# The last six row tiles of an FFN output product, regrouped into seven block products

## The chip, the cores and the metric

The kernel runs on one core of a Trainium2 chip. The metric is device time in microseconds (us): the median of three runs. Beside the runs there is one profiled execution, whose trace gives the start and the duration of every instruction on each engine: PE (TensorE, matrix products; PEld is its weight load), DVE (VectorE), ACT (ScalarE), POOL (GpSimd), and SP, whose queue issues most transfers.

## What is computed

Two layers of an encoder on 512 tokens of width 1024. Each layer is a token mixer of three branches, then an FFN with a gate, each followed by a residual sum and a layer norm. Only the end of the FFN matters here:

```python
u = jnp.einsum('bsd,df->bsf', x, w_ffn_in[l])
u_gate, u_up = jnp.split(u, 2, axis=-1)
ffn = jnp.einsum('bsf,fd->bsd', jax.nn.silu(u_gate) * u_up, w_ffn_out[l])
x = _layer_norm(DEEPNORM_ALPHA * x + ffn, ln2_g[l], ln2_b[l])
```

The hidden width is 2816, which is 22 row tiles of 128. So the FFN's output product is (512 tokens x 2816) times (2816 x 1024).

## The kernel before

**Products.** All values are float32. A product of two float32 operands is carried by splitting each into a high and a low part and adding three matmuls, high by high, high by low and low by high (`mm3`, lines 121 to 124). A weight block is therefore loaded by SP into a staging buffer (pool `wst`, 4 buffers), cast to its high part by ACT and reduced to its low part by a DVE subtraction (`Wt.split`, lines 154 and 155; `Staged`, lines 259 and 260). The pairs live in the pool `wsp`, with 3 buffers (`AHEAD`): the block of an item can be split only when the item three places ahead of it has left PE.

**Seven products instead of eight.** A group of row tiles of `w_ffn_out` is cut in two halves by rows (`kh` tiles each) and in two halves by columns (512 each); the tokens are cut in two halves of 256. A plain product of such a 2x2 by 2x2 arrangement takes eight block products. `fout_items` (line 1316) takes seven, named m1, y, x, m2, v, g and h, on sums of blocks. A block product is `product` (line 337): for each token tile `j` of 128 (two of them), `kh` times three matmuls into one PSUM bank. The sums of weight blocks are made by transfers that add to a staging buffer (`more`, line 177, on POOL's queue). The class `Chain` (line 191) holds one such buffer `a` from m1 to h, and another, `c`, for g. The sums of activation blocks are made by `Quarters.parts` and `Quarters.sums` (lines 279 and 289) on ACT and DVE, through the scheduled function `s_hid` (line 1214). Each finished block product is added into the residual tiles `z` by `plus` (line 1305), one DVE instruction of 128x512 for each use. There are eight `z` tiles: four token tiles `t`, two column halves `hf` each. m1 is added to one place and kept by an ACT copy, y is kept by an ACT copy, x takes five DVE instructions for each token tile (a subtraction, an addition, three of `plus`), g is added at two places, m2, v and h at one.

**The plan before.** `GROUPS` has two groups of eight row tiles, 0 to 7 (`o`) and 8 to 15 (`w`). The row tiles 16 to 21 (`REST`) are multiplied plainly by `fout_rest` (line 1367): for column half 0, a block of four and a block of two row tiles, whose four banks are added to `z` at the end; for column half 1, `chase`, which finishes one token tile after the other with 18 matmuls and closes the tile's norm behind each. In layer 1 (the last), closing a token tile is `Norm.finish` (line 475): `bn_stats` is done by `plus` with `final`, then an aggregate, a sum, a power on POOL, two DVE instructions that subtract the mean and multiply by the gain, two that multiply by the inverse deviation and add the bias, and the transfers of the result. In layer 0 it is `Norm.normalise` (line 488), which has two DVE instructions behind the power; then `Norm.transposes` (line 497) and `to_T` (line 517) turn the token tiles 0 and 1 for the next layer, and its first products follow (`u_first`, `halves`, line 711, with the other two token tiles turned by `hook`).

**The order.** The work is a list of items (line 1404). `run_items` (line 554) walks it: it fetches the weight blocks of the items up to two places ahead, runs the item, and runs the groups of functions that hang on the item between its products or after them (`between`). A scheduler in the language then orders the instructions of each engine from that order and from what is ready; on the chip each engine runs its own list in order.

Of the kernel before, what the change touches and what calls it, by code (L numbers as in the profile page):

```python
# [15 lines left out]
ALU = mybir.AluOpType  # L16
# [4 lines left out]
NT = S // P  # L21
# [8 lines left out]
FT = FFN // P  # L30
# [17 lines left out]
AHEAD = 3  # L48
NSTAGE = 4


GROUPS = [(0, 4), (8, 4)]
REST = 16


@with_exitstack
def trunk(ctx, tc, x_in, xT_in, w_in, ret_norm_g, da_norm_g, lq1, lk1, lq2, lk2, w_a, w_b, w_c, b_merge, w_out,
# [25 lines left out]
    def bank(name="ps"):  # L83
        return psp.tile([P, 512], F32, tag="ps", name=name)
# [31 lines left out]
    def split(pr, src, cols=slice(None), scale=None):  # L116

        part_hi(pr.hi[:, cols], src, scale)
        part_lo(pr.lo[:, cols], src, pr.hi[:, cols], scale)
# [71 lines left out]
    class Chain(Halves):  # L191
# [23 lines left out]

        def h(self):
            return self.block(self.__dict__.pop("a"))

    class Close(Halves):

# [144 lines left out]
    def proj_N(act, wts, t, ps, k0=0, start=True, stop=True):  # L365

        sl = slice(P * t, P * t + P)
        rows = [(wt, k) for wt in wts for k in range(wt.nk)]
        for i, (wt, k) in enumerate(rows):
            a = act[k0 + i]  # L370
            mm3(ps, a.hi[:, sl], a.lo[:, sl], wt.hi[:, k], wt.lo[:, k], start and i == 0, stop and i == len(rows) - 1)

    def rows_of(w, c, k0=0, nk=KT):

        return [([w[P * k:P * min(k + 4, k0 + nk), c:c + 512]], min(4, k0 + nk - k)) for k in range(k0, k0 + nk, 4)]
# [80 lines left out]
    def bcast_rows(src):  # L456

        r = [g(name="bc") for _ in range(2)]
        for hf in range(2):
            nc.sync.dma_start(r[hf], src[:, 512 * hf:512 * hf + 512].to_broadcast([P, 512]))  # L460
        return r
# [80 lines left out]
    def item(specs, fn, *groups):  # L542

        items.append((specs, fn, groups))
# [62 lines left out]
    def layer(l):  # L607
# [595 lines left out]
        def ffn_done(i, pg, pu):  # L1203
            t = g(name="fth")
            nc.scalar.activation(t, pg, AF.Tanh, scale=0.5)
            nc.vector.scalar_tensor_tensor(t, t, 1.0, pg, op0=ALU.add, op1=ALU.mult)
            nc.vector.tensor_mul(t, t, pu)  # L1207
            if i >= REST:
                hid[i] = Pair("hid")
                split(hid[i], t, scale=0.5)  # L1210
            else:
                hid[i] = t

        def s_hid(k):

            def fn():
                r0, kh = GROUPS[1]
                t1, t2 = hid[r0 + k], hid[r0 + kh + k]
                hid[r0 + k], hid[r0 + kh + k] = Quarters(), None
                hid[r0 + k].parts(t1, t2, 0.5)  # L1220
                hid[r0 + k].sums(t1, t2, 0.5)
            return fn
# [58 lines left out]
        def u_fin(pb):  # L1281

            return u_two(Chain(w_ffn_in[l], 0, 4, (512 * pb, FFN + 512 * pb)), x1q,
                         functools.partial(gate_half, pb), functools.partial(gated, pb))
# [20 lines left out]
        def plus(t, hf, ps, op, final=False):  # L1305

            z = x1["z"][t][hf]
            if (t, hf) in x2["fresh"]:
                x2["fresh"].remove((t, hf))
                nc.vector.scalar_tensor_tensor(z, z, ALPHA, ps, op0=ALU.mult, op1=op)  # L1310
            else:
                nc.vector.tensor_tensor(z, z, ps, op=op)  # L1312
            if final:
                x2["n"].stats(t, hf)

        def fout_items(gi):

            r0, kh = GROUPS[gi]
            hv = Chain(w_ffn_out[l], r0, kh)
            w = {}  # L1320

            def run(name, j, wt):
                return product([hid[r0 + k] for k in range(kh)], name, j, wt)

            def m1(wt):
                if gi == 0:
                    load_res(saved[2 * l])
                    x2["fresh"] = {(t, hf) for t in range(NT) for hf in range(2)}
                for j in range(2):
                    ps = run("m1", j, wt)  # L1330
                    w[j] = g(name="w")
                    nc.scalar.copy(w[j], ps)
                    plus(j, 0, ps, ALU.add)

            def y(wt):
                for j in range(2):
                    ps = run("y", j, wt)
                    w["y", j] = g(name="wy")
                    nc.scalar.copy(w["y", j], ps)

            def x(wt):
                for j in range(2):
                    ps = run("x", j, wt)
                    u = w.pop(j)
                    nc.vector.tensor_sub(u, ps, u)
                    plus(2 + j, 0, u, ALU.subtract)
                    nc.vector.tensor_add(u, u, w.pop(("y", j)))
                    plus(2 + j, 1, u, ALU.add)
                    plus(j, 1, u, ALU.add)

            def one(name, i, hf, op):
                def fn(wt):
                    for j in range(2):
                        plus(2 * i + j, hf, run(name, j, wt), op)
                return fn

            def gg(wt):
                for j in range(2):
                    ps = run("g", j, wt)
                    plus(2 + j, 1, ps, ALU.add)  # L1360
                    plus(2 + j, 0, ps, ALU.subtract)

            return {"c": hv.ahead_c, "m1": ([hv.m1], m1), "y": ([hv.y], y), "x": ([hv.x], x),
                    "m2": ([hv.m2], one("m2", 0, 0, ALU.add)), "v": ([hv.v], one("v", 0, 1, ALU.add)),
                    "g": ([hv.g], gg), "h": ([hv.h], one("h", 1, 0, ALU.add))}

        def fout_rest(hf):


            banks = {}  # L1370
            specs = rows_of(w_ffn_out[l], 512 * hf, REST, FT - REST)

            def block(kb):
                def fn(wt):
                    if kb == 0:
                        x2["n"] = Norm(x1["z"], v["g2"], v["b2"], bcast_rows(ln2_g[l:l + 1]),
                                       bcast_rows(ln2_b[l:l + 1]), xTs[l + 1], out if last else saved[2 * l + 1], xfs[l + 1])
                        banks[0] = [bank("pf") for _ in range(NT)]
                    end = kb == len(specs) - 1
                    for t in range(NT):  # L1380
                        proj_N(hid, [wt], t, banks[0][t], REST + 4 * kb, kb == 0, end)
                        if end:
                            plus(t, 0, banks[0][t], ALU.add, True)
                return fn

            def chase(*wts):
                n = x2["n"]
                for t in range(NT):
                    ps = bank("pf")
                    proj_N(hid, wts, t, ps, REST)  # L1390
                    if t in (1, 2) and not last:
                        n.transposes(t - 1)
                    plus(t, 1, ps, ALU.add, True)
                    if last:
                        n.finish(t)
                    else:
                        n.normalise(t)
                        if t == 2:
                            n.to_T(0)

            return [([sp], block(kb)) for kb, sp in enumerate(specs)] if hf == 0 else [(specs, chase)]

        p, q, o, w = u_fin(0), u_fin(1), fout_items(0), fout_items(1)
        for (specs, fn), *groups in [
            (u_ffn_first([8, 9]), [s_natural(0)], [s_x1(0)]), (u_ffn(10), [s_x1(1), s_x1(2)], [s_x1(3), s_natural(1)]),
            (p["m1"], [s_natural(2)], [p["c"], s_natural(3)]), (u_ffn(11),), (p["y"],), (p["m2"],),
            (p["v"],), (p["x"],), (u_ffn(12), [], [s_turn(0, 0)]), (p["g"],), (p["h"],),
            (q["m1"], [], [q["c"]]), (u_ffn(13), [s_turn(0, 1)]), (q["y"],), (q["m2"],),
            (q["v"],), (q["x"],), (u_ffn(14), [], [s_turn(1, 0)]), (q["g"],), (q["h"], [s_ready(0)], [s_ready(1)]),
            (o["m1"], [], [s_turn(1, 1)]), (u_ffn(15), [s_twins(0)], [s_twins(1), o["c"]]), (o["m2"],), (o["y"],), (u_ffn(16),),  # L1410
            (o["v"],), (o["x"],), (u_ffn(17),), (o["g"], [], [s_hid(0)]), (o["h"], [], [s_hid(1)]), (u_ffn(18), [s_hid(2)], [s_hid(3)]),
            (w["m1"],), (u_ffn(19), [], [w["c"]]), (w["m2"],), (w["y"],), (u_ffn(20),),
            (w["v"],), (w["x"],), (u_ffn(21),), (w["g"],), (w["h"],),
        ]:
            item(specs, fn, *groups)
        for it in fout_rest(0) + fout_rest(1):
            item(*it)

        def hook(b):
            x2["n"].transposes_of(1, b)  # L1420
# [56 lines left out]
```

## Time and profile before

| | us |
|---|---|
| median of three runs | 1895.63 (1895.56 to 1895.76) |
| the profiled execution | 1896.34 |
| its span, first to last instruction | 1894.5 |
| PE busy in the span | 1881.4 |
| DVE busy in the span | 1355.1 |
| ACT busy in the span | 946.2 |
| mean granted TensorE clock | 0.997 of full |

The span is 1.8 us shorter than the profiled execution's own time, which in turn is 0.7 us above the median of the runs. All times of day in this document are microseconds from the start of the span. A row of the timeline gives start, duration, engine, line, operation, what is written from what, the shape, how many instructions are merged into the row, and in brackets how long the engine stood idle before it and what released it. Durations of neighbouring instructions on one engine overlap, so what a queue can do is read from the distance of starts.

### The profile page before, as it was taken

How to read it: one execution, taken by the hardware profiler on the slowest of the kernel's cores; microseconds unless marked ns; L12 is line 12 of the kernel's file. 1: busy time of each engine (PE TensorE's matmuls, PEld its weight loads, DVE VectorE, ACT ScalarE, POOL GpSimd, SP SyncE). 2: the span in 40 equal slices, each digit the busy share in tenths (PEclk: the TensorE clock that was granted, in tenths of full speed). 3: DMA queues.
4: the chain of work that ended last, by engine and by line, in shares of the span. 5: the costliest groups of instructions: out<-in, count | busy, mean ns of one | idle time of the engine just before them, and what ended most of it. 6: DMA issues, size and time to landing. Idle time of an engine off the chain costs nothing. (4 is left out here: it accounts for less than half of the span.)

```text
span 1894.5 us, 24166 instructions
## 1 busy us (share of the span) xinstructions
PE 1881.4 (99%) x9170; PEld 1584.9 (84%) x9170; DVE 1355.1 (72%) x2159; ACT 946.2 (50%) x1575; POOL 113.9 (6%) x141
## 2 busy tenths in 40 slices
PE   9999999999999999999999999999999999999998
PEld 7888888888888888888898888888888898888886
DVE  6788867577765866786687788666776668667866
ACT  5555555566634444543255546555765344344430
POOL 2000000000000000000010000000000000000000
PEclk9999999999999999999999999999999999999999
DMA  9585443332155686765475944533322637777561
GB/s 282 170 268 152 122 159 108 122 122 68 57 186 147 156 178 169 207 156 127 139 190 171 285 113 145 169 104 95 123 79 73 205 101 175 181 179 196 139 153 45
DMA packets 239348, 285.11 MB, mean 150 GB/s; under 512 B 8580, under 2 KB 147936, under 8 KB 239232
## 3 DMA queue, kind: packets, MB, share of 16 engines
q1 hardware_dynamic: 215232, 237.01, 38.1%
q0 software_dynamic: 24000, 46.56, 14.4%
q8 instruction: 72, 1.18, 0.3%
q14 instruction: 44, 0.36, 0.1%
HBM read 260.42 MB, written 23.12 MB: 150 GB/s over the span
## 5 line engine op out<-in xcount | busy, mean ns | idle before, releaser
L122 PE MATMUL pt<-xTh,wh 128*128 128x512 f32 (+1 forms) x1328 | 497.2, 375 | 2.3 <-ACT wh L154 2.0
L124 PE MATMUL pt<-xTh,wl 128*128 128x512 f32 (+1 forms) x1328 | 494.0, 372 | 0.0
L123 PE MATMUL pt<-xTl,wh 128*128 128x512 f32 (+1 forms) x1328 | 493.9, 372 | 0.0
L154 ACT CAST wh<-st 128x1024 fp32r<-128x1024 f32 (+1 forms) x236 | 220.2, 962 | 210.4 <-PE pt L123 91.1
L155 DVE TENSOR_TENSOR wl<-st,wh 128x1024 fp32r<-128x1024 f32 (+1 forms) x236 | 257.4, 1111 | 81.0 <-ACT wh L154 75.0
L260 DVE TENSOR_TENSOR wl<-st,wh 128x2048 fp32r<-128x2048 f32 x98 | 224.4, 2290 | 117.2 <-ACT wh L259 116.8
L122 PEld LDWEIGHTS pt<-xTh,wh 128*128 128x128 f32 x1328 | 250.1, 189 | 44.3 <-ACT wh L154 2.5
L124 PEld LDWEIGHTS pt<-xTh,wl 128*128 128x128 f32 x1328 | 250.5, 189 | 43.9
L123 PEld LDWEIGHTS pt<-xTl,wh 128*128 128x128 f32 x1328 | 250.9, 189 | 41.9
L259 ACT CAST wh<-st 128x2048 fp32r<-128x2048 f32 x98 | 187.5, 1913 | 157.4 <-PE pf L124 73.9
L124 PE MATMUL pf<-wh,xTl 128*128 128x512 f32 x240 | 93.4, 389 | 0.0
L123 PE MATMUL pf<-wl,xTh 128*128 128x512 f32 x240 | 93.4, 389 | 0.0
L122 PE MATMUL pf<-wh,xTh 128*128 128x512 f32 x240 | 93.4, 389 | 0.0
L122 PE MATMUL pf<-wh,s43h 128*128 128x512 f32 x192 | 75.5, 393 | 0.1
L122 PE MATMUL pf<-wh,s12h 128*128 128x512 f32 x192 | 74.9, 390 | 0.0
L123 PE MATMUL pf<-wl,s43h 128*128 128x512 f32 x192 | 74.8, 389 | 0.0
L124 PE MATMUL pf<-wh,s12l 128*128 128x512 f32 x192 | 74.7, 389 | 0.0
L123 PE MATMUL pf<-wl,s12h 128*128 128x512 f32 x192 | 74.7, 389 | 0.0
L124 PE MATMUL pf<-wh,s43l 128*128 128x512 f32 x192 | 74.2, 390 | 0.0
L382 ACT COPY sw<-pt 32x512 f32<-32x512 f32 (+1 forms) x96 | 55.7, 580 | 29.2 <-PE pt L124 28.0
L1207 DVE TENSOR_TENSOR fth<-fth,pt 128x512 f32<-128x512 f32 x28 | 19.2, 687 | 56.5 <-PE pt L124 56.2
L124 PEld LDWEIGHTS pf<-wh,xTl 128*128 128x128 f32 x240 | 45.1, 188 | 9.4
(362 smaller groups left out, 3570.7 us busy)
## 6 DMA issues: line engine op xcount, KB each, us to landing
st<-in_w_in SPq DMA_DIRECT2D x60, 1024.0 KB, 5.4
st<-in_w_ffn_in SPq DMA_DIRECT2D x56, 512.0 KB, 5.6
st<-in_w_ffn_out SPq DMA_DIRECT2D x20, 1024.0 KB, 5.0
st<-in_w_in SPq DMA_DIRECT2D x32, 512.0 KB, 5.0
st<-in_w_ffn_in SPq DMA_DIRECT2D x16, 1024.0 KB, 5.8
st<-in_w_ffn_in POOLq DMA_DIRECT2D x16, 1024.0 KB, 9.1
st<-in_w_ffn_out POOLq DMA_DIRECT2D x16, 1024.0 KB, 8.6
st<-in_w_in POOLq DMA_DIRECT2D x12, 1024.0 KB, 11.8
```

The costliest lines, as they stand in the source:

```text
L122: nc.tensor.matmul(ps, lh, rh, start=start, stop=False)
L123: nc.tensor.matmul(ps, lh, rl, start=False, stop=False)
L124: nc.tensor.matmul(ps, ll, rh, start=False, stop=stop)
L154: return [nc.scalar.copy(self.hi[:, a:b], self.st[:, a:b]), nc.vector.tensor_sub(self.lo[:, a:b], self.st[:, a:b], f(self.hi[:, a:b]))]
L155: nc.vector.tensor_sub(self.lo[:, a:b], self.st[:, a:b], f(self.hi[:, a:b]))]
L259: nc.scalar.copy(self.hi, st)
L260: nc.vector.tensor_sub(self.lo, st, f(self.hi))
L382: nc.scalar.copy(sw[half * b:half * b + half], ps[half * o:half * o + half])
L1207: nc.vector.tensor_mul(t, t, pu)
```

## The change

The row tiles 16 to 21 become a third group of `GROUPS`, with `kh` = 3, called `r` in the list. Its seven products replace `fout_rest`. Its blocks are taken by a new class `Fore`: m1 is loaded by itself, and the held buffer `a` is loaded and added to ahead of it. The `w` and `r` products are interleaved in a new order. The norm object is made by r's m1; `plus` takes the statistics in r's m2, v, g and h; r's v closes the token tiles 0 and 1, r's h closes 2 and 3. In layer 0 the token tiles 0 and 1 are turned beside w's h. The hidden tiles 16 to 21 are no longer split one by one in `ffn_done`; `s_hid` splits and sums them for the group.

```diff
-GROUPS = [(0, 4), (8, 4)]
-REST = 16
+GROUPS = [(0, 4), (8, 4), (16, 3)]
...
+    class Fore(Chain):
+        def ahead_a(self):
+            self.a = self.load(0, 0)
+            self.more(self.a, 0, 1)
+
+        def m1(self):
+            return self.block(self.load(0, 0))
...
-            if i >= REST:
-                hid[i] = Pair("hid")
-                split(hid[i], t, scale=0.5)
-            else:
-                hid[i] = t
+            hid[i] = t
...
-            hv = Chain(w_ffn_out[l], r0, kh)
+            end = gi == len(GROUPS) - 1
+            hv = (Fore if end else Chain)(w_ffn_out[l], r0, kh)
...
+                if end:
+                    x2["n"] = Norm(x1["z"], v["g2"], v["b2"], bcast_rows(ln2_g[l:l + 1]),
+                                   bcast_rows(ln2_b[l:l + 1]), xTs[l + 1], out if last else saved[2 * l + 1], xfs[l + 1])
...
+            def normed(t):
+                (x2["n"].finish if last else x2["n"].normalise)(t)
+
+            def one(name, i, hf):
                 def fn(wt):
                     for j in range(2):
-                        plus(2 * i + j, hf, run(name, j, wt), op)
+                        plus(2 * i + j, hf, run(name, j, wt), ALU.add, end)
+                        if end and name != "m2":
+                            normed(2 * i + j)
+                        between()
                 return fn
 
             def gg(wt):
                 for j in range(2):
                     ps = run("g", j, wt)
-                    plus(2 + j, 1, ps, ALU.add)
+                    plus(2 + j, 1, ps, ALU.add, end)
                     plus(2 + j, 0, ps, ALU.subtract)
...
-        def fout_rest(hf):
...
+        def s_norm(t):
+            def fn():
+                if not last:
+                    x2["n"].transposes(t)
+                    if t:
+                        x2["n"].to_T(0)
+            return fn
+
+        p, q, o, w, r = u_fin(0), u_fin(1), fout_items(0), fout_items(1), fout_items(2)
...
-            (o["v"],), (o["x"],), (u_ffn(17),), (o["g"], [], [s_hid(0)]), (o["h"], [], [s_hid(1)]), (u_ffn(18), [s_hid(2)], [s_hid(3)]),
-            (w["m1"],), (u_ffn(19), [], [w["c"]]), (w["m2"],), (w["y"],), (u_ffn(20),),
-            (w["v"],), (w["x"],), (u_ffn(21),), (w["g"],), (w["h"],),
+            (o["v"],), (o["x"],), (u_ffn(17),), (o["g"], [], [s_hid(1, 0)]), (o["h"], [], [s_hid(1, 1)]),
+            (u_ffn(18), [s_hid(1, 2)], [s_hid(1, 3)]),
+            (w["m1"],), (u_ffn(19),), (w["y"],), (u_ffn(20),), (w["x"], [s_hid(2, 0), r["a"]]),
+            (u_ffn(21), [s_hid(2, 1), w["c"]]), (w["m2"], [s_hid(2, 2)]), (w["v"],),
+            (r["m1"],), (r["y"],), (w["g"], [], [r["c"]]), (r["m2"],), (r["x"],), (r["v"],),
+            (w["h"], [s_norm(0)], [s_norm(1)]), (r["g"],), (r["h"],),
         ]:
             item(specs, fn, *groups)
-        for it in fout_rest(0) + fout_rest(1):
-            item(*it)
```

More of the change, by code (lines that the diff above doesn't have):

```diff
@@ L1207, in ffn_done, with s_hid @@
             nc.vector.tensor_mul(t, t, pu)
-            if i >= REST:
-                hid[i] = Pair("hid")
-                split(hid[i], t, scale=0.5)
-            else:
-                hid[i] = t
-        def s_hid(k):
+            hid[i] = t
+        def s_hid(gi, k):
             def fn():
-                r0, kh = GROUPS[1]
+                r0, kh = GROUPS[gi]
                 t1, t2 = hid[r0 + k], hid[r0 + kh + k]
@@ L1349, in x @@
                     plus(j, 1, u, ALU.add)
-            def one(name, i, hf, op):
+            def normed(t):
+                (x2["n"].finish if last else x2["n"].normalise)(t)
+            def one(name, i, hf):
                 def fn(wt):
                     for j in range(2):
-                        plus(2 * i + j, hf, run(name, j, wt), op)
+                        plus(2 * i + j, hf, run(name, j, wt), ALU.add, end)
+                        if end and name != "m2":
+                            normed(2 * i + j)
+                        between()
                 return fn
@@ L1359, in gg @@
                     ps = run("g", j, wt)
-                    plus(2 + j, 1, ps, ALU.add)
+                    plus(2 + j, 1, ps, ALU.add, end)
                     plus(2 + j, 0, ps, ALU.subtract)
-            return {"c": hv.ahead_c, "m1": ([hv.m1], m1), "y": ([hv.y], y), "x": ([hv.x], x),
-                    "m2": ([hv.m2], one("m2", 0, 0, ALU.add)), "v": ([hv.v], one("v", 0, 1, ALU.add)),
-                    "g": ([hv.g], gg), "h": ([hv.h], one("h", 1, 0, ALU.add))}
-        def fout_rest(hf):
[L1370 to L1401, printed above, removed]
@@ L1403, in layer @@
-        p, q, o, w = u_fin(0), u_fin(1), fout_items(0), fout_items(1)
+            return {"c": hv.ahead_c, "a": getattr(hv, "ahead_a", None),
+                    "m1": ([hv.m1], m1), "y": ([hv.y], y), "x": ([hv.x], x), "m2": ([hv.m2], one("m2", 0, 0)),
+                    "v": ([hv.v], one("v", 0, 1)), "g": ([hv.g], gg), "h": ([hv.h], one("h", 1, 0))}
+        def s_norm(t):
[5 more added lines that the diff above has]
+            return fn
```

## The prediction

> **What bounds the kernel now.** I read the page's busy shares first, then the windows of the two ends of an FFN, then the timelines of PE and DVE there.
>
> ```profile
> span 1894.5 us, 24166 instructions
> PE 1881.4 (99%) x9170; PEld 1584.9 (84%) x9170; DVE 1355.1 (72%) x2159; ACT 946.2 (50%) x1575; POOL 113.9 (6%) x141
> ```
> ```profile
> 1740.00:1886.00 146.00, 145.83 (x641) 119.71 (x640) 104.88 (x146) 47.87 (x57) 8.03 (x7) 1.00 0.47 121
> 1853.00:1886.00 33.00, 32.83 (x145) 26.84 (x143) 21.53 (x36) 3.15 (x4) 2.90 (x3) 1.00 0.08 32
> ```
>
> The columns of a window are PE, PEld, DVE, ACT, POOL, granted clock, DMA share, GB/s. PE is full. DVE has a quarter free over the last FFN's end (104.9 of 146), and a third in the plain product that is replaced (21.5 of 33). By these averages the change is a matter of PE alone. The timeline of PE gives what one matmul is worth:
>
> ```profile
> 1853.03 0.39 PE L122 MATMUL pf<-wh,hidh 128*128 128x512 f32 x1
> ...
> 1885.44 0.39 PE L124 MATMUL pf<-wh,hidl 128*128 128x512 f32 x1
> ```
>
> These are the first and the last of the plain product's 144 matmuls in layer 1 (4 token tiles, 2 halves, 6 row tiles, 3 each). The distance is 32.41 us for 143 steps: 0.2267 us a step, though one lasts 0.39. PE's own end is 1885.44 + 0.23 = 1885.67. But what ends last is DVE:
>
> ```profile
> 1882.45 0.68 DVE L1312 TENSOR_TENSOR z<-z,pf 128x512 f32<-128x512 f32 x1
> ...
> 1886.85 0.68 DVE L1312 TENSOR_TENSOR z<-z,pf 128x512 f32<-128x512 f32 x1
> 1887.57 0.69 DVE L473 BATCH_NORM_STATS2 bn<-z 128x6 f32<-128x512 f32 x1
> 1888.30 0.21 DVE L478 BATCH_NORM_AGGREGATE mv<-bn 128x2 f32<-128x12 f32 x1
> 1888.54 0.15 DVE L480 TENSOR_SCALAR rs<-mv 128x1 f32<-128x1 f32 x1
> 1888.61 1.41 DVE L483 SCALAR_TENSOR_TENSOR z<-z,mv,bc 128x512 f32<-128x512 f32 x2
> 1889.93 1.41 DVE L485 SCALAR_TENSOR_TENSOR z<-z,rs,bc 128x512 f32<-128x512 f32 x2
> ```
>
> Closing a token tile takes DVE a cycle of 1886.85 - 1882.45 = 4.40 us, and 18 matmuls give it one every 4.08. The last cycle starts 1.2 us behind PE's end, and 7.65 us later the span is over (1894.5). The end of layer 1 is thus already DVE's, by a little.
>
> **The change part by part.** *PE.* Seven products of 2 token tiles, 3 row tiles, 3 matmuls: 126 in place of 144. 18 x 0.2267 = 4.08 us less in each layer, 8.16 in both, if PE never waits.
>
> *DVE, in sum.* Prices are distances of starts:
>
> ```profile
> 1774.46 0.42 DVE L114 SCALAR_TENSOR_TENSOR q<-fth,q 128x256 fp32r<-128x256 f32 x1
> 1774.80 0.68 DVE L114 SCALAR_TENSOR_TENSOR q2l<-fth,q2h 128x512 fp32r<-128x512 f32 x1
> 1775.40 0.42 DVE L292 TENSOR_TENSOR sa<-fth 128x256 f32<-128x256 f32 x1
> ...
> 1830.79 1.38 DVE L1345 TENSOR_TENSOR w<-pf,w 128x512 f32<-128x512 f32 x2
> 1832.08 1.29 DVE L1312 TENSOR_TENSOR z<-z,w 128x512 f32<-128x512 f32 x2
> 1833.28 1.29 DVE L1347 TENSOR_TENSOR w<-w,wy 128x512 f32<-128x512 f32 x2
> 1834.48 2.49 DVE L1312 TENSOR_TENSOR z<-z,w 128x512 f32<-128x512 f32 x4
> 1836.89 2.28 DVE L260 TENSOR_TENSOR wl<-st,wh 128x2048 fp32r<-128x2048 f32 x1
> 1839.09 0.68 DVE L1206 SCALAR_TENSOR_TENSOR fth<-fth,pt 128x512 f32<-128x512 f32 x1
> ...
> 1854.36 2.36 DVE L155 TENSOR_TENSOR wl<-st,wh 128x1024 fp32r<-128x1024 f32 x2 [0.44 <-ACT wh L154]
> 1864.76 1.29 DVE L155 TENSOR_TENSOR wl<-st,wh 128x512 fp32r<-128x512 f32 x2 [8.05 <-ACT wh L154]
> ```
>
> A 128x256 instruction steps 0.34, a 128x512 one 0.60, w's x 6.1 in all (1830.79 to 1836.89), a 2048-wide weight subtraction 2.20. The 1536-wide one of `r` is not in the trace; it lies between 1.18 (half the merged 1024-wide row) and 2.20. I take 1.67, two thirds of the way from 0.60 at 512 to 2.20 at 2048, as its width is; 0.5 either way on the two that count below would be 1 us of the range. Removed in a layer: six splits of hidden tiles (3.6), weight subtractions 7.0, eight `plus` (4.8). Added: three `s_hid` (each five of 0.34 and three of 0.60, 10.5), seven weight subtractions (11.7), 22 instructions of 128x512 on the products (m1 2, x 10, m2 2, v 2, g 4, h 2: 13.2). Net +20 us. By the average that fits: 104.9 + 20 of 141.9. `s_hid` fits indeed, as w's products cover it (DVE's 8.05 us of idle before 1864.76 was near there). What counts is when the rest may start.
>
> *The end of layer 1.* If PE never waits it ends at 1885.67 - 4.08 = 1881.59. Backwards, with 18 matmuls (4.08) for a product of `r` and 24 (5.44) for w's h: r.h starts at 1877.51, r.g 1873.43, w.h 1867.99, r.v 1863.91, r.x 1859.83. A block is split when the block three items ahead leaves PE, as ACT's row shows with PE as its releaser:
>
> ```profile
> 1831.51 1.91 ACT L259 CAST wh<-st 128x2048 fp32r<-128x2048 f32 x1 [1.68 <-PE pf L124]
> ```
>
> So w.h's block is cast from 1859.9 (r.m2 has left) to 1861.8, and DVE takes it to 1864.0. Behind it stands, all due by then or soon: r.x 6.1 (its first result is there at 1862.1), r.g's block 1.67, r.v with two closings 8.8, r.h's block 1.67, w.h's two `plus` 1.2, r.g with two `plus` and one statistic for each token tile 3.9, r.h's first closing 4.4. Sum 27.7: the last closing starts at 1891.7, against 1886.85. If independent instructions fill the gaps inside the chains, a closing is 4.2 and g 3.6, and it is 1890.8. Nothing of the sum can be earlier, since each block waits for its buffer and each result for PE. So layer 1 ends **3.9 to 4.9 us later**; I take 4.4. r.h's block comes after 1882, so PE waits some 4.8 us for it, which costs nothing more: DVE is still at w.h and r.g then.
>
> *Layer 0.* Here a closing is shorter, and what follows is not the end but the next layer's products:
>
> ```profile
> 932.16 0.69 DVE L1312 TENSOR_TENSOR z<-z,pf 128x512 f32<-128x512 f32 x1
> ...
> 934.69 1.00 DVE L495 TENSOR_SCALAR z<-z,mv,rs 128x512 f32<-128x512 f32 x2 [0.68 <-POOL rs L493]
> 936.25 0.69 DVE L1312 TENSOR_TENSOR z<-z,pf 128x512 f32<-128x512 f32 x1 [0.56 <-PE pf L124]
> ...
> 942.55 0.41 DVE L112 TENSOR_TENSOR xTl<-xf,xTh 128x256 fp32r<-128x256 f32 x1
> ```
> ```profile
> 941.02 1.03 PE L504 MATMUL px<-ident,z 128*128 128x128 f32 x8
> 945.99 0.28 PE L122 MATMUL pt<-xTh,wh 128*128 128x256 f32 x1
> ```
>
> A closing is 932.16 to 935.69, 3.5 us, with a hole of 0.68 where DVE waits for POOL. PE turned to the next layer at 945.99; without waits that becomes 941.91. The same queue, moved by 1885.67 - 945.99 = 939.68, has r.g's block done at 932.1, so r.v's closings end at 939.2, and r.h, due at 937.8, finds its block between 935.5 (subtracted in the first hole) and 940.8 (behind both closings). The turned tile follows 1.5 us behind the transposes (941.02 to 942.55), against 5.0 us of cover now. PE therefore waits 0 to 3 us; a hole in a queue that has ready work is filled, so I take 1. Layer 0: -4.1 to -1.1, taken **-3.1**. Behind it DVE is 6 us later than now, and the half-width products of 17 us and more hide that.
>
> *Transfers.*
>
> ```profile
> st<-in_w_ffn_out SPq DMA_DIRECT2D x20, 1024.0 KB, 5.0
> st<-in_w_ffn_out POOLq DMA_DIRECT2D x16, 1024.0 KB, 8.6
> ```
>
> Nine transfers of 768 KB replace four blocks in a layer. w's `a`, r's `a` and `c` hold three of four staging buffers from w.g on, so r.m2's and r.v's blocks share one. r's `c` is loaded when w.g's block is split, about 1846, and takes 5.0 + 8.6 us at most: there by 1860, due at 1863.9. Additions queue on POOL ahead of the powers, the last near 1854, well before the first power. I cost all of it at nothing; were `c` late by one more addition, 8.6 us, it would come at 1868.5, while DVE is at r.x until 1870.1.
>
> *A rule against this sum.* DVE's rows overlap: four instructions of 0.68 take 2.49. The Trainium skill, "VectorE: DVE Perf Modes", section "The DRAIN you can't avoid", says that the next instruction does not start until the pipe is empty; the trace differs, starts are 0.60 apart where durations are 0.68. Were it so for the 36 wide instructions of the sum, 36 x 0.08 = 2.9 us would be added, and the time would be near 1899.8; as the row shows the overlap, I give this no chance of its own.
>
> **The sum.** 4.4 - 3.1 = **+1.3 us**. On the profiled execution (1896.34) 1897.6, on the median 1896.9. The parts' ends give -0.2 to +3.8, 1895.4 to 1899.4.
>
> **The rivals.** *PE alone decides*: both layers keep their 4.08, DVE's queue drains in time, and the tail behind PE stays 7.65 + 1.2. -8.2 us, 1887.5. For it: PE's 99%, DVE's free quarter. Against it: 27.7 us of DVE work that cannot start before 1864.0, with PE's end at 1881.6. The Trainium skill, "Perfetto Trace Analysis", section "Identifying the Most-Contended Engine", says to optimise the engine of the highest occupancy first, which gives this time; its next section adds that a kernel can have regimes. 0.06. *Half of it*: layer 0 keeps all and DVE's tail grows by less than two blocks' subtractions (1.67 + 2.2 less): -4.1 + 0.5 = -3.6, 1892.0. 0.10. *Layer 0 stalls too*, the slower end: r.h's block stands behind both closings (3 us of waiting), and then the next layer's two weight blocks (about 2.3 each) stand behind r.g's `plus` and before r.h's closings, so that PE waits again for one of them. From the point where r.h's block is not split before 937.8. Layer 0 then goes to between 0 and +3, with layer 1's 4.4: 1900 to 1903, I say 1901. For it: DVE's queue there is full from 922 on. Against it: its holes, and the 945.99 row, where PE went on without a gap while blocks were still being split. 0.24.
>
> **How the numbers follow.** A measurement of this kernel tells about 0.2%, 3.8 us, from no change: faster is below 1891.8, slower above 1899.4. Forecast 1896.9 with 0.60; the rivals have 0.06, 0.10 and 0.24. Faster 0.06, same 0.60 + 0.10 = 0.70, slower 0.24. The range 1892.0 to 1902.0 leaves out the first rival and the upper half of the last, under 0.2.
>
> **What would show it.** In layer 1: DVE without a hole from r.x to the end, the last `plus` of a closing 9 to 11 us behind where PE would have ended, and PE waiting 4 to 5 us before r.h's first matmul, released by DVE. In layer 0: PE's first product of the next layer 3 us earlier than 945.99. PE's busy time falls by 8.2. I am wrong if the closings of layer 1 keep pace with PE, or if PE in layer 0 has holes before r.h or behind it of more than 3 us.

## The result, and the profile after

| | before | after |
|---|---|---|
| median of six runs each | 1895.01 us (1893.60 to 1895.76) | 1901.82 us (1901.19 to 1903.09) |
| the profiled execution | 1896.34 | 1901.65 |
| its span | 1894.5 | 1899.9 |

The ratio after to before is 1.0037, with a 95% interval of 1.0024 to 1.0050. The changed kernel is slower by about 7 us, where +1.3 was forecast. The page of the changed kernel, and windows over the same two stretches as before:

```profile
span 1899.9 us, 24193 instructions
PE 1874.6 (99%) x9134; PEld 1579.8 (83%) x9134; DVE 1391.4 (73%) x2221; ACT 962.5 (51%) x1593; POOL 124.4 (7%) x149
```
```profile
1853.00:1886.00 33.00, 31.09 (x138) 25.40 (x136) 30.31 (x44) 8.28 (x6) 4.55 (x4) 1.00 0.49 124
1740.00:1886.00 146.00, 144.09 (x636) 118.99 (x634) 118.64 (x167) 58.34 (x67) 12.31 (x11) 1.00 0.62 149
```

PE works 6.8 us less, with 36 matmuls fewer. DVE works 36.3 us more. In the window from 1853 to 1886 DVE goes from 21.5 to 30.3 busy: 92%, beside a page that still says 73% for the whole. To compare positions one sentence is needed: the profile of before started with PE at a lower clock (0.91 granted over its first 20 us, 1.00 in the profile after), and the same early work stands 2.4 us earlier from the span's start in the profile after (the first 96 matmuls of one product start at 31.04 before, at 28.60 after).

**Layer 1** ends later, as forecast, though by less. PE has no wait at all there and ends at 1883.70 + 0.23; DVE has no hole from w.h's block to the end:

```profile
1883.70 0.39 PE L122 MATMUL pf<-wh,q2l 128*128 128x512 f32 x1
```
```profile
1864.40 2.27 DVE L268 TENSOR_TENSOR wl<-st,wh 128x2048 fp32r<-128x2048 f32 x1
1866.59 1.28 DVE L1354 TENSOR_TENSOR w<-pf,w 128x512 f32<-128x512 f32 x2
...
1872.60 1.75 DVE L268 TENSOR_TENSOR wl<-st,wh 128x1536 fp32r<-128x1536 f32 x1
...
1876.77 1.71 DVE L268 TENSOR_TENSOR wl<-st,wh 128x1536 fp32r<-128x1536 f32 x1
...
1888.67 1.27 DVE L1316 TENSOR_TENSOR z<-z,pf 128x512 f32<-128x512 f32 x2
...
1895.38 1.41 DVE L493 SCALAR_TENSOR_TENSOR z<-z,rs,bc 128x512 f32<-128x512 f32 x2
```

The rows are w.h's block, r.x, r.g's block, r.h's block (slipped in between r.v's statistics and its first closing), the additions of r.h's two results, and the very last DVE work. PE's end stands 2.34 us later than the prediction's 1881.59, which is layer 0's doing and the start's. Taken from there the layer ends 1899.9 - 2.34 - 1894.5 = 3.1 us later than before.

**Layer 0** is where the forecast fails. The timeline of PE around w.h and the granted clock (the sixth figure behind the window's length, after the five engines):

```profile
926.38 0.39 PE L122 MATMUL pf<-wh,q2l 128*128 128x512 f32 x1
933.31 1.97 PE L512 MATMUL px<-ident,z 128*128 128x128 f32 x8 [6.55 <-DVE z L503]
934.93 0.78 PE L120 MATMUL pf<-wh,q2h 128*128 128x512 f32 x1
935.50 0.63 PE L121 MATMUL pf<-wl,q2h 128*128 128x512 f32 x1
...
939.19 0.39 PE L122 MATMUL pf<-wh,q2l 128*128 128x512 f32 x1
939.42 1.03 PE L512 MATMUL px<-ident,z 128*128 128x128 f32 x8
...
948.47 0.28 PE L120 MATMUL pt<-xTh,wh 128*128 128x256 f32 x1
```
```profile
926.00:934.00 8.00, 1.45 (x7) 0.99 (x6) 7.76 (x14) 0.00 (x0) 0.70 (x2) 0.85 0.52 166
934.00:936.00 2.00, 2.00 (x9) 1.81 (x9) 1.00 (x2) 0.00 (x0) 0.39 (x1) 0.50 1.08 380
936.00:938.00 2.00, 2.00 (x6) 1.58 (x5) 0.00 (x0) 0.00 (x0) 0.00 (x0) 0.50 0.18 57
...
940.00:945.00 5.00, 5.00 (x26) 4.21 (x24) 4.43 (x7) 4.12 (x8) 0.00 (x0) 1.00 0.12 12
```

PE has done w.h's first token tile at 926.61 and stands until 933.31: 6.7 us. What it stands at is not a product. It is the eight transposes of token tile 0, which the plan puts between the two token tiles of w.h, and they need the tile closed and normalised by DVE. After the pause the clock is at 0.50. The eight transposes take 1.62 instead of the 0.79 of the second set, and the next twelve matmuls 4.49 instead of 2.72: another 2.6 us. Together that is 9.3 us of loss, against the 4.1 that the shorter products save. PE turns to the next layer at 948.47, which with the 2.4 of the start is 4.9 later than before's 945.99 (the sum gives 5.2). And DVE in the same stretch:

```profile
917.87 2.29 DVE L268 TENSOR_TENSOR wl<-st,wh 128x2048 fp32r<-128x2048 f32 x1
920.08 1.28 DVE L1354 TENSOR_TENSOR w<-pf,w 128x512 f32<-128x512 f32 x2
...
926.10 1.75 DVE L268 TENSOR_TENSOR wl<-st,wh 128x1536 fp32r<-128x1536 f32 x1
927.76 1.28 DVE L1316 TENSOR_TENSOR z<-z,pf 128x512 f32<-128x512 f32 x2
928.96 1.28 DVE L481 BATCH_NORM_STATS2 bn<-z 128x6 f32<-128x512 f32 x2
...
930.26 1.71 DVE L268 TENSOR_TENSOR wl<-st,wh 128x1536 fp32r<-128x1536 f32 x1
...
932.71 1.00 DVE L503 TENSOR_SCALAR z<-z,mv,rs 128x512 f32<-128x512 f32 x2
```

DVE has no hole from w.h's block to there. It starts r.v's first closing only at 927.76, because w.h's block, r.x (6.0 us) and r.g's block stand ahead in its list, and it normalises token tile 0 at 932.71.

By the traces the loss is 4.9 in layer 0 and 3.1 in layer 1, 8.0 together; the medians say 6.8, or 7.7 against the 1894.15 that before took among the runs of the first experiments.

### The profile page after: what moved, and what is told of

It is laid out like the page before. It is cut to its first block, busy times and chain, and to the rows that moved or that the text cites. A ratio compares the mean times of both kernels' runs of the same rounds, so it can differ in the third digit from the quotient of the medians.

```text
span 1899.9 us, 24193 instructions
## 1 busy us (share of the span) xinstructions
PE 1874.6 (99%) x9134; PEld 1579.8 (83%) x9134; DVE 1391.4 (73%) x2221; ACT 962.5 (51%) x1593; POOL 124.4 (7%) x149
## 5 line engine op out<-in xcount | busy, mean ns | idle before, releaser
L268 DVE TENSOR_TENSOR wl<-st,wh 128x2048 fp32r<-128x2048 f32 (+1 forms) x112 | 248.8, 2221 | 113.2 <-ACT wh L267 112.6
L267 ACT CAST wh<-st 128x2048 fp32r<-128x2048 f32 (+1 forms) x112 | 208.2, 1859 | 184.2 <-PE pf L122 69.2
L153 DVE TENSOR_TENSOR wl<-st,wh 128x1024 fp32r<-128x1024 f32 (+1 forms) x220 | 243.0, 1122 | 66.7 <-ACT wh L152 60.5
L152 ACT CAST wh<-st 128x1024 fp32r<-128x1024 f32 (+1 forms) x220 | 208.3, 971 | 155.9 <-PE pt L121 58.8
L120 PE MATMUL pf<-wh,s43h 128*128 128x512 f32 x216 | 84.9, 393 | 0.0
L120 PE MATMUL pf<-wh,s12h 128*128 128x512 f32 x216 | 84.2, 390 | 0.0
L121 PE MATMUL pf<-wl,s43h 128*128 128x512 f32 x216 | 84.1, 390 | 0.0
L122 PE MATMUL pf<-wh,s12l 128*128 128x512 f32 x216 | 84.1, 389 | 0.0
L121 PE MATMUL pf<-wl,s12h 128*128 128x512 f32 x216 | 84.1, 389 | 0.0
L390 ACT COPY sw<-pt 32x512 f32<-32x512 f32 (+1 forms) x96 | 55.6, 579 | 27.1 <-PE pt L122 25.9
L176 POOL DMA_DIRECT2D st<-in_w_ffn_out x24 | 30.8, 1297 | 349.8 <-DVE wl L268 226.7
```

The lines of the kernel that those rows point to most:

```text
L120: nc.tensor.matmul(ps, lh, rh, start=start, stop=False)
L121: nc.tensor.matmul(ps, lh, rl, start=False, stop=False)
L122: nc.tensor.matmul(ps, ll, rh, start=False, stop=stop)
L152: return [nc.scalar.copy(self.hi[:, a:b], self.st[:, a:b]), nc.vector.tensor_sub(self.lo[:, a:b], self.st[:, a:b], f(self.hi[:, a:b]))]
L153: nc.vector.tensor_sub(self.lo[:, a:b], self.st[:, a:b], f(self.hi[:, a:b]))]
L176: nc.gpsimd.dma_start(t, self.src(i, j), accum_op=ALU.add)
```

## The experiments

Names used in the expectations: "the record" is the prediction above. Theory B is its sum. Theory A, formed on reading the trace, is that the place of the turning (the transposes inside w.h) and the half clock behind it are the loss of layer 0. Theory C is that DVE's queue is the loss, and that the place only decides where PE meets it. Theory D is used in two senses, each told in the expectation that has it. Ratios are to before, with 95% intervals. One is no different from 1 where its interval holds 1.

### Each layer alone

The third group in one layer only; the other keeps the plain product and the order of before.

```diff
-            hid[i] = t
+            if l not in THIRD and i >= REST:
+                hid[i] = Pair("hid")
+                split(hid[i], t, scale=0.5)
+            else:
+                hid[i] = t
...
+        ] + (plan_third if l in THIRD else plan_rest):
+            item(specs, fn, *groups)
+        for it in [] if l in THIRD else fout_rest(0) + fout_rest(1):
+            item(*it)
```

With THIRD = (0,), layer 0 alone:

> The third group in layer 0 alone; layer 1 keeps the plain product of before. Theory A (from the two traces): layer 0 loses what it saves and more at the transposes that stand inside w's h, 4.1 us less of matmuls and 9.2 us of waiting, so +5.1 us against the kernel before; PE's hole is the one of the changed kernel, 6 to 7 us ahead of the first transposes. Theory B (the recorded sum): layer 0 gains 3.1 us (-4.1 to -1.1) and all the loss is in layer 1, so -3 us.

Measured: 1898.69 against 1894.15, +4.5; ratio 1.0026 [1.0016, 1.0035]. PE stands in the same place:

```profile
935.25 1.97 PE L514 MATMUL px<-ident,z 128*128 128x128 f32 x8 [6.54 <-DVE z L505]
```

With THIRD = (1,), layer 1 alone:

> The third group in layer 1 alone. Theory A: the closing of the token tiles by DVE makes the end 3.1 us later, as the difference of the two traces behind the start of layer 1 has it. Theory B (the recorded sum): 4.4 us later (3.9 to 4.9). A third view, that DVE's free quarter hides it and only layer 0 matters: 4.1 us faster. DVE should have no hole from r.x to the end, and PE none before r.h.

Measured: 1896.71 against 1894.15, +2.6; ratio 1.0010 [1.0001, 1.0019]. The two add to 7.1, about the whole. The traces give the same split where the start plays no part. From the first transposes behind the token mixer of layer 0 (583.78 in after) to those of layer 1 (1530.21) are 941.1 us in before, 946.4 in after, 946.1 with layer 0 alone and 941.2 with layer 1 alone; from there to the end are 367.2, 369.7, 366.9 and 369.6. So the layers add up, the record's layer 0 (-3.1) has the wrong sign, and its layer 1 (+4.4) is 1.3 to 1.9 too large.

### The turning moved behind w.h

```diff
-            (w["h"], [s_norm(0)], [s_norm(1)]), (r["g"],), (r["h"],),
+            (w["h"],), (r["g"], [s_norm(0)]), (r["h"], [s_norm(1)]),
```

> The changed kernel, with the two sets of transposes of layer 0 moved: the first behind r.g, the second between the two token tiles of r.h. Theory A (PE's queue is in order, and only the place of the transposes makes it wait): PE has r.g to do meanwhile and turns to the next layer near 939 instead of 948.5; of these 9.4 us up to 3 may come back because the turned tiles are then later than the products that need them: 1892.4 to 1895.4 where the changed kernel has 1901.8. Theory C (DVE's queue is simply too long in layer 0, and PE waits for it wherever the transposes stand): less than 3 us gained, above 1898.8.

Measured: 1901.13, ratio 1.0037 [1.0025, 1.0050], against after's 1901.82: no gain that a measurement tells. PE no longer stands in w.h, r.g and r.h run through to 938.82 + 0.23, and then it stands at the first products of the next layer. PE's timeline there, and DVE's:

```profile
941.09 0.36 PE L120 MATMUL pt<-xTh,wh 128*128 128x256 f32 x1 [1.88 <-DVE z L1316]
945.06 0.58 PE L120 MATMUL pt<-xTh,wh 128*128 128x256 f32 x1 [3.61 <-DVE z L1316]
946.25 0.58 PE L120 MATMUL pt<-xTh,wh 128*128 128x256 f32 x1 [0.61 <-DVE z L1316]
```
```profile
935.13 4.62 DVE L153 TENSOR_TENSOR wl<-st,wh 128x1024 fp32r<-128x1024 f32 x4
939.67 1.28 DVE L1316 TENSOR_TENSOR z<-z,pf 128x512 f32<-128x512 f32 x2
...
943.74 1.26 DVE L1316 TENSOR_TENSOR z<-z,pf 128x512 f32<-128x512 f32 x2
```

The releaser is the line of `plus`. Those additions empty the PSUM banks of w.h, r.g and r.h, and the next products need banks. They stand in DVE's queue behind four weight subtractions of the next layer (4.62 us). 6.1 us of waiting come back here, with matmuls at half clock behind them (steps of 0.21 where 0.12 is full). This is what theory C expected (above 1898.8): A, by itself, falls.

### The clock alone

64 transposes of the identity, ahead of the turning of token tile 0, keep PE busy through the pause.

```diff
+                    if t == 0:
+                        busy = bank("busy")
+                        for _ in range(64):
+                            nc.tensor.transpose(busy[:, :P], ident, ident)
                     x2["n"].transposes(t)
```

> The changed kernel with 64 more 128x128 transposes of the identity (about 6.3 us) in front of the first transposes of layer 0, which fill PE's hole and change nothing else. Theory D: PE's granted clock fell to a half because PE stood still, and 2.6 us of the 9.2 are matmuls at that clock; with PE kept busy the clock stays at 1.00 and the kernel gets 2.2 to 2.6 us faster (near 1899.4). Rival: the slow matmuls have another cause (a late bank, the transfers of that moment): no change, or slower by what the fill overhangs.

Measured: 1901.64, ratio 1.0039 [1.0026, 1.0051]. The five runs lie between 1899.61 and 1904.65, so the time alone cannot tell the expected 1899.4 from no gain; the trace has to. It shows the clock at 1.00 throughout, the twelve matmuls in 2.86 us, and PE at the next layer at 946.25, 2.2 us earlier than in after. Then, some 20 us on, a load takes it back:

```profile
946.25 0.28 PE L120 MATMUL pt<-xTh,wh 128*128 128x256 f32 x1
...
967.24 0.24 PE L643 MATMUL pcol<-ident,rows 64*128 64x64 f32 x1 [1.76 <-DMA rows<-in_ln_b]
967.41 0.38 PE L120 MATMUL pt<-xTh,wh 128*128 128x256 f32 x1
```

That 967.41 is 968.28 in after: 0.9 of the 2.2 are left. In this trace the half clock is a real loss where it happens, and PE meets a later wait when it goes. What sets the time of that load wasn't tried.

### The subtractions on another engine

In both layers, the low parts of r.v's, r.g's and r.h's blocks are subtracted by POOL.

```diff
-            nc.vector.tensor_sub(self.lo, st, f(self.hi))
+            (low or nc.vector).tensor_sub(self.lo, st, f(self.hi))
...
+        def v(self):
+            self.low = nc.gpsimd
+            return Chain.v(self)
```

> The changed kernel, with the low parts of r.v's, r.g's and r.h's weight blocks subtracted on POOL instead of DVE, in both layers. Theory C (DVE's queue is what is too long at the end of each layer): 3 x 1.67 = 5.0 us leave DVE's full stretch, layer 1 ends up to 5 us earlier, layer 0's hole of PE before the first transposes gets shorter by the same: 1892 to 1897 where the changed kernel has 1901.8. Rival: the place of the transposes alone costs layer 0 its time, then only layer 1 gains, 1897; or POOL's subtraction is slower than DVE's queue, then nothing or a loss.

Measured: 1910.64, ratio 1.0082 [1.0067, 1.0097], 9 us slower than after. Rows of POOL and of DVE in layer 1:

```profile
1871.49 3.76 POOL L274 TENSOR_TENSOR wl<-st,wh 128x1536 fp32r<-128x1536 f32 x1 [4.07 <-ACT wh L273]
1875.62 3.54 POOL L274 TENSOR_TENSOR wl<-st,wh 128x1536 fp32r<-128x1536 f32 x1 [0.36 <-ACT wh L273]
```
```profile
1871.21 4.59 DVE L1322 TENSOR_TENSOR z<-z,w 128x512 f32<-128x512 f32 x2
1875.73 4.58 DVE L1362 TENSOR_TENSOR w<-w,wy 128x512 f32<-128x512 f32 x2
```

POOL takes 3.5 to 3.8 us for what DVE does in 1.7, and two DVE additions with both inputs in SBUF take 4.6 together instead of 1.28 while it does. The Trainium skill, "SBUF — State Buffer", section "Who interferes with whom", says that a DVE instruction with two SBUF inputs contends with a GpSimd instruction that reads SBUF, the one blocking until the other is done; the rows agree. The same with the turning moved as well (the third experiment's edit):

> The transposes of layer 0 moved behind r.g and into r.h, and the three low parts on POOL. In the run with the late transposes alone, PE had no hole before them but then waited 7 us for banks that DVE had not emptied. Theory C: with 5.0 us less on DVE those waits shrink by about as much; together with layer 1's 5.0 it is 1891 to 1894. Rival: the next layer's own weight blocks on DVE and ACT set the pace there, then layer 0 gains less than 2 us and it is near 1896.

Measured: 1909.07, ratio 1.0076 [1.0059, 1.0093]. Work moved to POOL isn't taken off DVE, so neither run can test theory C.

### Less work for DVE in the closings

Layer 1's two instructions that subtract the mean and multiply by the gain are left out of every closing: of after, and of before.

```diff
-            for z, gam in zip(self.z[t], self.gam):
-                nc.vector.scalar_tensor_tensor(z, z, mv[:, 0:1], gam, op0=ALU.subtract, op1=ALU.mult)
```

> The changed kernel without the two instructions of each closing in layer 1 that subtract the mean and multiply by the gain: that part of the last norm is left out. If DVE ends layer 1 alone, its queue loses 4 x 1.32 = 5.3 us, and the end comes 5.3 us earlier (1896.5 for 1901.8). If PE or a transfer paced the closings, less than 3 us.

> The kernel before with the same two instructions of each closing in layer 1 left out. A closing then takes DVE 3.1 us, PE gives one every 4.08, so PE paces the end: the 1.2 us behind PE go, and 1.3 of the last closing: 2.3 us earlier, not 5.3.

Measured: 1898.41 for after without them, 3.4 less than after, which lies between the 5.3 and the "less than 3" of the expectation. From r.x to the end DVE takes 1895.40 - 1869.50 = 25.9 us:

```profile
1869.50 1.28 DVE L1352 TENSOR_TENSOR w<-pf,w 128x512 f32<-128x512 f32 x2
...
1892.66 2.74 DVE L491 SCALAR_TENSOR_TENSOR z<-z,rs,bc 128x512 f32<-128x512 f32 x4 [0.58 <-POOL rs L489]
```

In after it is 1896.79 - 1866.59 = 30.2: 4.3 of the 5.3 us that were taken out (four times 1.32). In before the same edit gives 1893.37 against 1894.09, ratio 0.9993 [0.9984, 1.0003]; that holds both no change and the expected 2.3, but not 5.3. There the closings follow PE:

```profile
1876.97 0.69 DVE L1310 TENSOR_TENSOR z<-z,pf 128x512 f32<-128x512 f32 x1
...
1881.05 0.69 DVE L1310 TENSOR_TENSOR z<-z,pf 128x512 f32<-128x512 f32 x1 [0.16 <-PE pf L124]
...
1885.13 0.69 DVE L1310 TENSOR_TENSOR z<-z,pf 128x512 f32<-128x512 f32 x1
```

They come 4.08 apart, PE's 18 matmuls. So DVE's work sets the end of layer 1 in after. In before, where the cycle of a closing is 4.40 beside PE's 4.08, it does so by a little, and with the two instructions left out PE sets the pace up to the last closing.

### The subtractions left out

The low part of a block of `r` becomes an ACT copy in place of the DVE subtraction (so the low part is not the remainder, and the subtraction is left out). First for r.v, r.g and r.h, then for all seven.

```diff
-            nc.vector.tensor_sub(self.lo, st, f(self.hi))
+            if low:
+                nc.scalar.copy(self.lo, st)
+            else:
+                nc.vector.tensor_sub(self.lo, st, f(self.hi))
```

> The changed kernel with the low parts of r.v's, r.g's and r.h's weight blocks written by an ACT copy of the block instead of the DVE subtraction: the subtraction is left out, the matmuls stay. ACT stands idle there and shares nothing with DVE that showed so far. Theory C (DVE's queue is too long at the end of both layers): 5.0 us less of DVE ahead of the first transposes of layer 0 (hole of 6.7 us to under 2, clock loss of 2.6 us gone or less) and 5.0 us in layer 1: 1889 to 1893 for 1901.8. Theory A (the place of the transposes): layer 0 keeps its hole, only layer 1 gains, 1896.8.

> The same for all seven blocks of r in both layers: 11.7 us less of DVE in each layer, the subtraction left out. If DVE's queue is the whole cause, what is left is the saving of PE: 1886 to 1889, 5 to 8 us under the kernel before. If something else holds too (transfers that feed the blocks, PSUM banks, the order of PE), it stays above 1890.

Measured: 1897.27, ratio 1.0013 [1.0004, 1.0022], and 1895.01, ratio 1.0005 [0.9996, 1.0015]. The first is 4.5 under after, the second 6.8 under it and no different from before. Both missed what theory C gave, 1889 to 1893 and 1886 to 1889. The first lies near theory A's 1896.8, but not in A's way: over the stretch of 946.4 us from layer 0 to layer 1 it is 3.7 shorter than after, and 2.3 shorter from there to the end, where A kept layer 0's hole and had all the gain in layer 1. With all seven these are 3.6 and 3.4. The rows of the second say why it gains no more: PE still stands in w.h, 926.47 to 930.47, and in layer 1 DVE is still full from w.h's block to the end (1889.72).

```profile
930.47 1.97 PE L518 MATMUL px<-ident,z 128*128 128x128 f32 x8 [3.84 <-DVE z L509]
...
944.86 0.28 PE L120 MATMUL pt<-xTh,wh 128*128 128x256 f32 x1
```

The same place in the first of the two runs:

```profile
932.16 1.97 PE L521 MATMUL px<-ident,z 128*128 128x128 f32 x8 [3.79 <-DVE z L512]
```

The wait in w.h went from 6.7 to 4.0 us in both: the four further copies change nothing there. What they gain is in layer 1. The two subtractions between w.h's block and the turned tile were r.g's and r.h's; what is left is r.x and the closing itself. The two edits together, all seven copies and the late turning:

> All seven low parts of r's blocks are an ACT copy (the subtraction left out, so DVE has 11.7 us less per layer), and layer 0 turns its token tiles beside r.g and r.h instead of inside w.h. The run before this one, with the copies but the turning inside w.h, gave 1895.0 with 4.2 us of standing in layer 0 and matmuls at half clock behind it. Theory C (DVE's queue is what lasts, the place of the turning only decides where PE meets it): with the subtractions gone DVE has about 6 us of room, so the place counts now: no hole in w.h, no half clock, PE turns to the next layer 3 to 5 us earlier than in that run (940 to 942 in place of 944.9), and the total is 1890 to 1892. Theory D (DVE is still full there from the closings and sums alone): the waiting shows again at the next layer's products, released by DVE's additions into z, as it did when the turning was moved by itself; total 1894 to 1896.

Measured: 1895.2, ratio 1.0003 [0.9994, 1.0013], the same as with the copies alone, in both stretches of the trace as well (942.8 and 366.3 us, beside 942.9 and 366.3). PE reaches the next layer at 939.56, 5.3 earlier than the run before, and there stands three times:

```profile
940.49 0.39 PE L120 MATMUL pt<-xTh,wh 128*128 128x256 f32 x1 [0.65 <-DVE z L1322]
941.68 0.38 PE L120 MATMUL pt<-xTh,wh 128*128 128x256 f32 x1 [0.80 <-DVE z L1322]
944.88 0.58 PE L121 MATMUL pt<-xTl,wh 128*128 128x256 f32 x1 [2.82 <-DVE xTl L110]
```
```profile
941.54 2.35 DVE L153 TENSOR_TENSOR wl<-st,wh 128x1024 fp32r<-128x1024 f32 x2
943.81 0.68 DVE L487 BATCH_NORM_STATS2 bn<-z 128x6 f32<-128x512 f32 x1
944.42 0.41 DVE L110 TENSOR_TENSOR xTl<-xf,xTh 128x256 fp32r<-128x256 f32 x1
```

4.3 us of waiting, all released by DVE, and half clock behind it. Theory D, in the sense of this expectation, holds: without a single subtraction of `r`, the sums, the closings and the next layer's blocks still keep DVE behind PE.

### Another order

r.m1 and r.y are put ahead of w.v and w.g, and r.x ahead of r.m2, so that r.x is off DVE earlier.

```diff
-            (w["m2"], [s_hid(2, 2)]), (w["v"],),
-            (r["m1"],), (r["y"],), (w["g"], [], [r["c"]]), (r["m2"],), (r["x"],), (r["v"],),
+            (w["m2"], [s_hid(2, 2)]), (r["m1"],),
+            (r["y"],), (w["v"],), (w["g"], [], [r["c"]]), (r["x"],), (r["m2"],), (r["v"],),
```

> The changed kernel in another order: r.m1 and r.y ahead of w.v and w.g, r.x ahead of r.m2, so that the added transfer for r.x has two more products to land in. In the changed kernel DVE had two holes of 2.0 and 2.7 us in layer 1 while ACT waited for transfers. If these holes count in full, 2 to 5 us faster in each layer's end, 1894 to 1899. If DVE's sum from r.x on decides alone, within 1 us of 1901.8.

Measured: 1913.15, ratio 1.0098 [1.0083, 1.0113], 11 us slower than after, which neither half of the expectation had. ACT stands for a transfer, and DVE behind it:

```profile
1871.90 4.64 ACT L267 CAST wh<-st 128x1536 fp32r<-128x1536 f32 x3 [11.88 <-DMA st<-in_w_ffn_out]
```
```profile
1873.41 1.76 DVE L268 TENSOR_TENSOR wl<-st,wh 128x1536 fp32r<-128x1536 f32 x1 [5.97 <-ACT wh L267]
```

As I read it, the four staging buffers are held longer in this order (r's `a` and `c`, w's `a`), so that the loads start late; that was not tried by itself. The record cost the transfers at nothing. In layer 1 of the change that held: DVE has no hole behind 1856.27, and w.h's block is done 0.25 us behind the time worked out. In this order it does not hold.

No version that computes the whole was faster than before.

## Why the prediction was wrong, point by point

- **What bounds the kernel**: right for layer 1. DVE sets its end, in before by a little and in after by much, and the two runs without the gain agree. PE's busy time fell by 6.8, not 8.2; the slow start of before's profile and the half clock in after's both lie in that difference, and they were not taken apart.
- **Layer 1, 3.9 to 4.9, taken 4.4**: right in that DVE's queue sets the end, too large in its size: 2.6 alone, 3.1 in the trace of the whole. The queue begins as worked out (w.h's block is done at 1866.59 - 2.34 = 1864.25, against 1864.0), and one 1536-wide subtraction steps 1.67 as estimated. But the sum took closings as chains of 4.4 that stand end to end. With two token tiles closing together, the hole of the one is filled with the other: from r.v's first addition (1874.27) to the next product's (1884.48) stand two closings, r.h's block (1.62) and one addition of w.h (0.6), which leaves 8.0 for the closings, not 8.8. From 1884.48 to the end are 12.3 us, where the sum has 1.2 + 3.9 + 2 x 4.4 - 0.6 = 13.3. Two signs that the record named did not come. PE does not wait 4 to 5 us before r.h, as r.h's block took such a hole at 1876.77. And the last addition of a product starts near 1889.3, 5.3 behind PE's end and not 9 to 11, as both closings of r.h come behind it together.
- **Layer 0, -4.1 to -1.1, taken -3.1**: the step that failed, by its sign: +4.5 alone. It read "PE therefore waits 0 to 3 us; a hole in a queue that has ready work is filled, so I take 1", and looked for that wait at r.h's block. DVE's queue was worked out well enough to tell the rest. In its own positions of layer 1, w.h's first token tile is done at 1867.99 + 2.72 = 1870.7. r.v's first addition cannot start before 1864.0 + 6.1 + 1.67 = 1871.8. A closing of 3.5 ends at 1875.3, 4.6 behind PE, and at 1876.9 with r.h's block filling the hole: 6.2, where 6.7 was measured. The record does not make that comparison: the place of the transposes in PE's queue, written in the plan as two groups of w.h, is in none of its steps. The rule of the filled hole worked against the layer: what filled it was r.h's block, and it delayed the tile that PE was waiting for.
- **The half clock** was in no term: 2.6 us behind the pause in layer 0. Its row is the 0.50 above. The Trainium skill, "TensorE: Matmul & The Clock Gate", section "What's actually happening", has the clock fall to half after an idle window of about 3.4 us; the trace agrees in kind, with 0.50 after 6.7 us. In the trace of the run that kept the clock up, part of the gain is lost again at a later wait, so this loss may not simply add.
- **The rival "Layer 0 stalls too"** had the right sign and nearly the right total (1901 against 1901.8), with a wait in another place. That its total is so near is luck: it has 4.4 for layer 1 and up to 3 for layer 0, where 2.6 and 4.5 were measured. Its second half, PE waiting for DVE at the next layer's products, is what the late turning brought out, though for banks and turned tiles rather than weight blocks.
- **The sign "PE in layer 0 has holes of more than 3 us"**, named beforehand as what would make the forecast wrong, is what the trace shows.
- **The rule against the sum** was rightly given no chance, but the trace does not differ from the page. The Trainium skill, "VectorE: DVE Perf Modes", adds in the same section, "The DRAIN you can't avoid", that a next instruction that is not held starts earlier; the starts 0.60 apart under durations of 0.68 agree with that.

What stays open: why the load of the norm's rows lands late enough to take back most of the 2.2 us in the run with the clock kept up, and how much of the second loss in the late turning belongs to the banks alone, and whether another order of DVE's own list (r.x ahead of w.h's block, for one) would shorten the waits.

## What to carry to other kernels

Before costing a change that gives one engine less and another more, list for each instruction that the first engine executes in order what it needs from the second, and set the two clocks side by side at each of those places, transposes included; a wait moved from one place came back at the next in the two pairs of runs shown here. An average of 73% says nothing about an engine that is full for the last 30 us of the kernel. Where one engine is short of time, test a cure by leaving its work out first: here, with the subtractions of `r` gone from DVE, the kernel only came level with before, so another engine that took them over would not by that alone have made the change a gain. The sums were left out nowhere and the closings not in layer 0; on them this is no answer.

## What the runs showed of the hardware that was not expected

- A subtraction of 128x1536 float32 takes POOL 3.5 to 3.8 us where DVE steps 1.67, and two DVE additions of 128x512 with both inputs in SBUF go from 1.28 to 4.59 us while it runs.
- After 6.7 us of standing, TensorE's granted clock is 0.50, and it is full again only some 5 us after work resumes (933.31 to about 938.5). After the 4.0 us of the two runs with ACT copies it is at half too, and full again 3.0 to 3.4 us after work resumes (932.16 to about 935.2, 930.47 to about 933.9).
